# The last half chunk of the delta rule on the attention's tiles, a solve in blocks of 16, and two pads

## Chip, cores, metric

One Trainium2 core runs the whole program. The metric is device microseconds (us) of one execution, with all inputs in HBM at the start and the result in HBM at the end. Engines are named as the profile names them: PE (TensorE matmuls), PEld (its weight loads), DVE (VectorE), ACT (ScalarE), POOL (GpSimd), SP (the queue that issues most DMAs).

## What is computed

One decoder layer over 2048 tokens of width 1024: a normalised input is projected once; a stick-breaking attention of 8 heads and a gated delta rule of 4 heads run side by side; their outputs are projected back, and a feed-forward of width 4096 follows.

```python
h = rmsnorm(x, norm_mix) * (1 + sc_a) + sh_a
proj = h @ w_in                     # q, k, v of the attention; q, k, v, z, a, b of the delta rule
o_a = stick_breaking_attention(q_a, k_a, v_a)
o_b = chunk_gated_delta_rule(q_b, k_b, v_b, g, beta)       # chunks of 64 tokens
x = x + g_a * (concat[o_a, rmsnorm(o_b) * silu(z)] @ w_out)
h = rmsnorm(x, norm_mlp) * (1 + sc_m) + sh_m
x = x + g_m * (relu(h @ w_ff1)^2 @ w_ff2)
# in the delta rule, for each head and chunk of 64 tokens:
a_mat = tril(k_beta @ k.T * decay, -1) + eye               # 64 x 64
t_mat = triangular_solve(a_mat, eye)                       # its inverse
```

## The kernel before

**Stages.** The sequence is cut into four chunks of 512 tokens, taken from c = 3 down to c = 0. For each one, `project(c)` multiplies the normalised input by the input weights (PE, tiles `mmk`, `mmv`, `mmq`, `mmK`, `mmQ`, `mmV`, `mmz`), `decay_terms(c)` prepares the decays, `delta_half(c, 1)` and `delta_half(c, 0)` run the delta rule over 256 tokens each, and `attention(c)` runs 4 pairs of heads in 2 groups each. `attention_far(c)` then reads a flag from the chip (line 567) and branches: the far keys are needed only if some weight hasn't died out. `outs(c)` (tiles `mmo`) is the output projection of a chunk: outs(3) runs in chunk 1, outs(2) beside chunk 0, outs(1) and outs(0) behind it. The feed-forward then takes tokens in two halves of 1024, first chunks 2 and 3: `load_h` makes the operand tiles `b..`, `ff1` multiplies w_ff1 by them (lines 1151 to 1153), `ff2` multiplies w_ff2 by the tiles `hidh`, `hidl` that `split` makes (lines 1210 to 1212). Each float32 product is three float32r matmuls (high by high, high by low, low by high) of 512 columns.

**Order.** Nothing is ordered by hand. A scheduler orders the instructions by their place in the program and what they depend on, and `tc.high_priority(offset=800)` moves a block's instructions up by 800 places. Each engine then runs its own list strictly in that order. Tiles of one tag share its buffers: a tile waits until an earlier user of the buffer is done.

**Tiles and pools.** On the right side of SBUF lie the pools `at` (the attention's tiles: `sn`, `ald`, `sp`, `aT0`, `aT1`, `qf`, `rkb`, `av`, `om`) and below it `dn` (the delta rule's: `dd`, `kw`, `ktok`, `mt`, `bv`, `AT`, `wq` and others, one buffer a tag, `cv` three). When chunk 0 is done, `right.close()` frees both, and the pool `fb` with the feed-forward's `b..` tiles (112 KB) takes the same room. Its tiles wait one by one for the tiles that they lie on. On the left lie `cp`, `wp` (weights: `ws`, `wh`, `wl`) and `act` (activations), then smaller pools, and in their room later the feed-forward's.

**Addresses.** The trace doesn't show them; they follow from the pools and sizes. Counted in bytes past a multiple of 256, tiles start in the kernel before at: `wp`, `act`, `hidh`, `hidl`: 32; the `b..` tiles and `at`: 224; most of `dn`: 64; `wab` (line 433): 128.

**A half chunk.** `delta_half` transposes k (line 720, `kt`), forms the lower matrix `mt` (lines 756, 758) for two blocks p = 1, 0 of 128 tokens, packs the 32 x 32 diagonal blocks into `Gt` (line 762) and transposes them into `M` (line 776). The **solve** (lines 787 to 793) inverts all of them at once on DVE: 31 steps of two or four small instructions each, 116 in a half chunk. `XT` and `xt` put the inverses back (lines 795, 798), eight transposes fill the block diagonal `xbd` (line 802). `pz` and `px` (lines 839, 845) join pairs of 32 to 64 on PE, `pw` and `pu` apply the inverse, and a recursion of four steps follows (lines 868 to 889), with a norm and the transfer to `mix_d` at the end (lines 892 to 907).

Of the kernel before, what the change touches and what calls it, by code (L numbers as in the profile page):

```python
# [16 lines left out]
P = 128  # L17
# [10 lines left out]
DH = 4  # L28
# [13 lines left out]
C_MASK = C_XI + 8 * 32  # L42
# [10 lines left out]
NVEC = 115  # L53
# [3 lines left out]
def tile_hybrid_layer(  # L57
# [23 lines left out]
    mx, pms, inner, right = [ctx.enter_context(ExitStack()) for _ in range(4)]  # L81
# [50 lines left out]
    if True:  # L132
# [7 lines left out]
        pq = inner.enter_context(tc.tile_pool(name="pq", bufs=2, space=PSUM))  # L140
        at = sb("at", 1, right, "right")
# [489 lines left out]
        for t in xbd + vz:  # L631
            G.memset(t, 0.0)
# [51 lines left out]
        def delta_half(c, hf, terms):  # L684
# [9 lines left out]
            def tile2(tag, name, bufs=1):  # L694
                return dn.tile(bc, F32, tag=tag, name=f"{name}{nm}", bufs=bufs)
# [7 lines left out]
            dd = [tile2(f"dd{p}", f"dd{p}_") for p in range(2)]  # L703
# [47 lines left out]
            Gt = dn.tile([P, 32, 2, DH], F32, tag="Gt", name=f"Gt{nm}")  # L751
# [23 lines left out]
            M = dn.tile([P, 32, 32], F32, tag="M", name=f"M{nm}")  # L775
            V.transpose(M, Gt.rearrange("q i p h -> q i (p h)").unsqueeze(2).to_broadcast([P, 32, 4, 8]))
            X = dn.tile([P, 8, 32], F32, tag="X", name=f"X{nm}")
            nc.sync.dma_start(X.rearrange("p a i -> p (a i)"), consts[:, C_XI:C_MASK])
            Xv = X.rearrange("p (e o) i -> p o e i", o=2)
            tm = dn.tile([P, 2, 80], F32, tag="tm", name=f"tm{nm}")  # L780
            for j in range(31, 0, -1):
                a0 = j // 4
                todo = []
                for o in range(2):
                    e0 = (a0 - o + 1) // 2
                    ne = 4 - e0
                    if ne:
                        todo.append((Xv[:, o, e0:4], tm[:, o, 0:ne * j].rearrange("p (e i) -> p e i", e=ne), ne))
                for x, t, ne in todo:
                    V.tensor_tensor(t, x[:, :, j:j + 1].to_broadcast([P, ne, j]),  # L790
                                    M[:, 0:j, j].unsqueeze(1).to_broadcast([P, ne, j]), ALU.mult)
                for x, t, ne in todo:
                    V.tensor_tensor(x[:, :, 0:j], x[:, :, 0:j], t, ALU.subtract)
            XT = dn.tile([P, 8, 4, 2, DH], F32, tag="Gt", name=f"XT{nm}")
            V.transpose(XT.rearrange("q a g p h -> q a (g p h)"), X)
            xt = [dn.tile([P, DH, 8, 4], F32, tag=f"xt{p}", name=f"xt{p}_{nm}") for p in range(2)]
            for p in (1, 0):
                (A.copy if p else G.tensor_copy)(xt[p], XT[:, :, :, p, :].rearrange("q a g h -> q h a g"))
                xt[p] = xt[p].rearrange("q h a g -> q h (a g)")
# [25 lines left out]
            wq = [dn.tile([P, DH, 2, P], F32, tag=f"wq{p}", name=f"wq{nm}_{p}") for p in range(2)]  # L825
# [7 lines left out]
            for p in (1, 0):  # L833
# [7 lines left out]
                for a in range(2):  # L841
                    lo, hi = slice(64 * a, 64 * a + 32), slice(64 * a + 32, 64 * a + 64)
                    ps = bank(f"px{nm}_{p}{a}", [P, DH, 32], "s")
                    for h in range(DH):
                        T.matmul(ps[hi, h, :], lhsT=zt[lo, h, :], rhs=xbd[p][lo, h, lo], start=True, stop=True)
                    A.activation(xbd[p][hi, :, lo], ps[hi], AF.Copy, scale=-1.0)
# [183 lines left out]
        for c in range(NCH - 1, -1, -1):  # L1030
# [210 lines left out]
def _layout(inputs):  # L1241
# [30 lines left out]
    xi = np.zeros((P, 8, 32), np.float32)  # L1272
    for p in range(P):
        for a in range(8):
            xi[p, a, 4 * a + p % 32 // 8] = 1
    cst[:, C_XI:C_MASK] = xi.reshape(P, 256)
# [47 lines left out]
```

## Time and profile before

| | us |
|---|---|
| median of 3 runs | 2852.66 |
| lowest, highest | 2842.65, 2853.85 |
| the profiled execution | 2854.61 |
| its span in the trace | 2852.8 |
| granted TensorE clock, mean of the span | 0.964 |

The span splits at 1497 us: before it lies everything up to the output projection, behind it the feed-forward, in which PE is busy without a break but for one stretch around 2150 us. A row "line engine op out<-in xcount" names the line of the kernel, the tile written and the tiles read; "idle before" is the time that the engine stood still ahead of it, with what ended that.

### The profile page before, as it was taken

To read this page: it belongs to the slowest core of one execution; us is meant where nothing else is said; L and a number is where in the kernel's file an instruction comes from. 1 tells how busy PE (TensorE), PEld (TensorE's weight loads), DVE (VectorE), ACT (ScalarE), POOL (GpSimd) and SP (SyncE) were. 2 spreads that over 40 slices of the span, in tenths; PEclk is the share of its full clock that TensorE was granted. 3 is DMA by queue.
4 is the path that set the end of the run, shared out by engine and by line. 5 is a ranking of instruction groups with operands and counts; after the bars stand their busy time and mean duration, and the time that the engine had idled before them with its cause. 6 is when DMAs were issued, how large, how long until landed. Compare 5 with 4: busy or idle time off the path is not lost.

```text
span 2852.8 us, 37490 instructions
## 1 busy us (share of the span) xinstructions
PE 2631.5 (92%) x13044; PEld 2135.1 (75%) x13044; DVE 1775.0 (62%) x4290; ACT 1165.0 (41%) x2263; POOL 659.5 (23%) x525
## 2 busy tenths in 40 slices
PE   4898789899979999799859999999998999999999
PEld 2687568777868778677648888888876888888887
DVE  7664993588346873568566556555668555555655
ACT  4553443154415452354344343344345343344332
POOL 3222300121002100022253222222226222222221
PEclk9999889999989999898979999999999999999999
DMA  8786786565556556554342111111024111111012
GB/s 308 265 311 207 251 293 208 183 191 176 184 158 205 182 176 189 158 181 138 122 161 94 59 60 42 48 60 60 30 100 166 60 59 43 47 60 60 30 60 89
DMA packets 219089, 390.21 MB, mean 137 GB/s; under 512 B 21944, under 2 KB 68984, under 8 KB 214776
## 3 DMA queue, kind: packets, MB, share of 16 engines
q1 hardware_dynamic: 200696, 358.16, 38.8%
q10 hardware_dynamic: 18176, 29.37, 2.8%
q8 instruction: 110, 1.80, 0.3%
q14 instruction: 107, 0.88, 0.1%
HBM read 302.94 MB, written 84.51 MB: 136 GB/s over the span
## 4 chain that ended last, share of the span: by engine, by line
PE 47%; DVE 2%; DMA 2%; issue 1%; POOL 1%; ACT 0%; SPq 0%; DVEq 0%; POOLq 0%; ACTq 0%
PE f L1210 8%; PE f L1211 8%; PE f L1212 8%; PE f L1151 7%; PE f L1152 7%; PE f L1153 7%; DMA fx<-x_d 1%; DVE fx L1067 0%; DVE bl L130 0%; PE mmo L216 0%; PE mmo L218 0%; PE mmo L217 0%; DVE y L1215 0%; DMA mx<-mix_d 0%; DMA rs_d<-acc 0%
## 5 line engine op out<-in xcount | busy, mean ns | idle before, releaser
L1215 DVE SCALAR_TENSOR_TENSOR y<-f,mods,y 128x512 f32<-128x512 f32 x512 | 363.6, 746 | 249.3 <-PE f L1212 249.1
L1210 PE MATMUL f<-hidh,wh 128*128 128x512 f32 x1024 | 401.5, 393 | 7.1 <-DVE y L1215 7.1
L1211 PE MATMUL f<-hidl,wh 128*128 128x512 f32 x1024 | 401.8, 393 | 3.2 <-POOL hidl L1193 3.2
L1212 PE MATMUL f<-hidh,wl 128*128 128x512 f32 x1024 | 381.2, 392 | 0.8 <-POOL wl L173 0.8
L1151 PE MATMUL f<-bh,swh 128*128 128x512 f32 x896 | 354.9, 396 | 16.6 <-ACT swh L1144 16.6
L1152 PE MATMUL f<-bl,swh 128*128 128x512 f32 x896 | 354.3, 395 | 0.0
L1153 PE MATMUL f<-bh,swl 128*128 128x512 f32 x896 | 347.4, 395 | 0.0
L1210 PEld LDWEIGHTS f<-hidh,wh 128*128 128x128 f32 x1024 | 193.7, 189 | 54.1 <-DVE y L1215 11.4
L1211 PEld LDWEIGHTS f<-hidl,wh 128*128 128x128 f32 x1024 | 193.8, 189 | 44.7 <-POOL hidl L1193 4.4
L1212 PEld LDWEIGHTS f<-hidh,wl 128*128 128x128 f32 x1024 | 193.4, 189 | 42.7 <-POOL wl L173 1.3
L1151 PEld LDWEIGHTS f<-bh,swh 128*128 128x128 f32 x896 | 168.4, 188 | 57.9 <-ACT swh L1144 17.0
L172 ACT CAST wh<-ws 128x512 fp32r<-128x512 f32 x128 | 79.5, 621 | 301.1 <-PE f L1211 245.6
L1152 PEld LDWEIGHTS f<-bl,swh 128*128 128x128 f32 x896 | 168.4, 188 | 41.6 <-issue 0.2
L1153 PEld LDWEIGHTS f<-bh,swl 128*128 128x128 f32 x896 | 168.1, 188 | 41.2
L1193 POOL TENSOR_TENSOR hidl<-t,hidh 128x512 fp32r<-128x512 f32 x64 | 101.6, 1587 | 335.6 <-ACT hidh L1192 316.0
L1144 ACT CAST swh<-wa 128x512 fp32r<-128x512 f32 x96 | 59.4, 622 | 263.0 <-PE f L1152 258.9
L1165 DVE TENSOR_TENSOR t<-t,f 128x512 f32<-128x512 f32 x128 | 87.4, 683 | 121.8 <-PE f L1153 88.8
L1137 POOL TENSOR_TENSOR sws<-wa 128x512 f32<-128x512 f32 x64 | 90.4, 1412 | 307.6 <-DVE wl L173 285.2
L1145 DVE TENSOR_TENSOR swl<-sws,swh 128x512 fp32r<-128x512 f32 x128 | 144.9, 1133 | 20.7 <-ACT swh L1144 20.6
L1145 DVE TENSOR_TENSOR swl<-wa,swh 128x512 fp32r<-128x512 f32 x96 | 86.3, 901 | 94.5 <-ACT swh L1144 94.5
L173 POOL TENSOR_TENSOR wl<-ws,wh 128x512 fp32r<-128x512 f32 x52 | 67.6, 1301 | 248.8 <-ACT wh L172 248.4
L1166 ACT ACTIVATE t<-t 128x512 f32<-128x512 f32 x128 | 80.9, 632 | 81.2 <-DVE t L1165 81.2
(354 smaller groups left out, 5866.1 us busy)
## 6 DMA issues: line engine op xcount, KB each, us to landing
wa<-in_w_ff_dram SPq DMA_DIRECT2D x32, 1024.0 KB
ws<-in_w_ff_dram SPq DMA_DIRECT2D x128, 256.0 KB
wada<-in_w_ada_dram SPq DMA_DIRECT2D x48, 512.0 KB
wso<-in_w_out_dram SPq DMA_DIRECT2D x64, 256.0 KB
cv_d<-ev SPq DMA_DIRECT2D x48, 256.0 KB
cv<-cv_d SPq DMA_DIRECT2D x24, 512.0 KB
x<-in_xc_dram SPq DMA_DIRECT2D x40, 256.0 KB
mx<-mix_d SPq DMA_DIRECT2D x32, 256.0 KB
```

Of the source, the lines that this page charges most:

```text
L1137: G.tensor_tensor(t, x, y, op)
L1145: V.tensor_tensor(wl, x, wh.bitcast(F32), SUB)
L1151: T.matmul(ps, lhsT=wh[:, k, :], rhs=ah, start=first and k == 0, stop=False, skip_group_check=True)
L1152: T.matmul(ps, lhsT=wh[:, k, :], rhs=al, start=False, stop=False, skip_group_check=True)
L1153: T.matmul(ps, lhsT=wl[:, k, :], rhs=ah, start=False, stop=stop and k == 3, skip_group_check=True)
L1165: V.tensor_tensor(t, t, ps, op)
L1166: A.activation(t, t, AF.Relu)
L1193: (G if i % 2 else V).tensor_tensor(hl, x, hh.bitcast(F32), SUB)
L1210: T.matmul(ps[n], lhsT=wh[:, s], rhs=ah, start=j == 0, stop=False)
L1211: T.matmul(ps[n], lhsT=wh[:, s], rhs=al, start=False, stop=False)
L1212: T.matmul(ps[n], lhsT=wl[:, s], rhs=ah, start=False, stop=j == 1)
L1215: V.scalar_tensor_tensor(ys[m][:, cs], ps[n], mods[:, 40 + m:41 + m], ys[m][:, cs], ALU.mult, ALU.add)
```

## The change

- The order for chunk 0: `delta_half(0, 1)`, `attention(0)`, `attention_far(0)`, then `delta_half(0, 0)`, in place of both half chunks ahead of the attention. Both keep the offset of 800.
- In that last half chunk, `dd`, `kw`, `ktok`, `mt`, `bv`, `AT` and `wq` are taken from tags of `at` (the dict `free`); all other tiles stay in `dn`.
- In all eight half chunks the solve inverts 16 x 16 blocks: two of them lie side by side in `M`, selected by two 0/1 columns of `vecs`; 15 steps of two instructions; then pairs of 16 are joined to 32 on PE (`py`, `pv`), with more copies on ACT and four whole transposes on DVE, while `xbd` is filled by ACT.
- Two pads of 56 floats (224 bytes) for a partition: `pad` at the start of `cp` on the left, `edge` at the outer end of the right side, which stays until the end of the program. With them and the new tile sizes tiles start, past a multiple of 256, at: `wp`, `act`, `hidh`, `hidl`: 0; the `b..` tiles: 0; `at` but for its first tile: 0; `dn`: 224.

```diff
-C_MASK = C_XI + 8 * 32
+C_MASK = C_XI + 8 * 16
...
-NVEC = 115
+V_E0 = 115
+NVEC = 117
...
+    cp.tile([P, 56], F32, name="pad")
...
+        edge = right_pad.enter_context(tc.tile_pool(name="edge", bufs=1, side="right"))
+        edge.tile([P, 56], F32, name="edge")
         at = sb("at", 1, right, "right")
         dn = sb("dn", 1, right, "right")
...
+        yz = [dn.tile([P, DH, 32], F32, name=f"yz{i}") for i in range(2)]
...
+            free = {"mt1": ("aT0", 1), "mt0": ("aT1", 1), "bv1": ("av", 2), "bv0": ("av", 2), "AT1": ("ald", 2),
+                    "AT0": ("ald", 2), "ktok1": ("qf", 2), "ktok0": ("qf", 2), "kw1": ("om", 1), "kw0": ("rkb", 1),
+                    "wq1": ("sp", 2), "wq0": ("sp", 2)} if (c, hf) == (0, 0) else {}
...
+                if tag in free:
+                    return at.tile(shape, F32, tag=free[tag][0], name=f"{name}{nm}", bufs=free[tag][1])
...
+            if free:
+                dd = at.tile([P, 2, DH, P], F32, tag="sn", name=f"dd{nm}")
+                dd = [dd[:, p] for p in range(2)]
...
-                    (A.copy if p else G.tensor_copy)(Gt[q, :, p, :], mt[p][q, :, q].rearrange("q h i -> q i h"))
+                    for e in range(2):
+                        (A.copy if p else G.tensor_copy)(Gt[q, :, e, p, :],
+                                                              mt[p][q, :, 32 * d + 16 * e:32 * d + 16 * e + 16]
+                                                              .rearrange("q h i -> q i h"))
...
+            M = dn.tile([P, 16, 32], F32, tag="M", name=f"M{nm}")
+            V.transpose(M, Gt.rearrange("q i e p h -> q i (e p h)").unsqueeze(2).to_broadcast([P, 16, 2, 16]))
+            e0, e1 = vecs[:, V_E0:V_E0 + 1], vecs[:, V_E0 + 1:V_E0 + 2]
+            V.tensor_scalar(M[:, :, 16:32], M[:, :, 16:32], e1, None, ALU.mult)
+            V.scalar_tensor_tensor(M[:, :, 0:16], M[:, :, 0:16], e0, M[:, :, 16:32], ALU.mult, ALU.add)
...
+            for j in range(15, 0, -1):
+                n = 8 - j // 2
+                x, t = X[:, j // 2:], tm[:, 0:n * j].rearrange("p (e i) -> p e i", e=n)
+                V.tensor_tensor(t, x[:, :, j:j + 1].to_broadcast([P, n, j]),
+                                M[:, 0:j, j].unsqueeze(1).to_broadcast([P, n, j]), ALU.mult)
+                V.tensor_tensor(x[:, :, 0:j], x[:, :, 0:j], t, ALU.subtract)
+            Xw = dn.tile([P, 8, 32], F32, tag="Xw", name=f"Xw{nm}")
+            V.tensor_scalar(Xw[:, :, 0:16], X, e0, None, ALU.mult)
+            V.tensor_scalar(Xw[:, :, 16:32], X, e1, None, ALU.mult)
...
             for p in (1, 0):
...
+                for e in range(2):
+                    A.copy(xt[p][:, :, 16 * e:16 * e + 16].rearrange("q h (a g) -> q h a g", g=2),
+                           XT[:, :, :, e, p, :].rearrange("q a g h -> q h a g"))
+                turned(xr[p], xt[p])
+                ps = bank(f"py{nm}_{p}", [P, DH, 16], "s")
                 for d in range(4):
                     q = slice(32 * d, 32 * d + 32)
-                    V.transpose(xbd[p][q, :, q], xt[p][q])
+                    for h in range(DH):
+                        T.matmul(ps[q, h, :], lhsT=mt[p][q, h, q], rhs=xt[p][q, h, 16:32], start=True, stop=True)
+                A.copy(yz[p][:, :, 16:32], ps)
+                ps = bank(f"pv{nm}_{p}", [P, DH, 16], "s")
...
+                        T.matmul(ps[q, h, :], lhsT=yz[p][q, h, :], rhs=xr[p][q, h, 0:16], start=True, stop=True)
+                V.tensor_tensor(xr[p][:, :, 0:16], xr[p][:, :, 0:16], ps, ALU.subtract)
+                turned(xt[p], xr[p])
+                for d in range(4):
+                    q = slice(32 * d, 32 * d + 32)
+                    A.copy(xbd[p][q, :, q], xr[p][q])
...
                 delta_half(c, 1, terms)
-                delta_half(c, 0, terms)
+                if c:
+                    delta_half(c, 0, terms)
             with tc.high_priority(offset=800 if c == 0 else 1):
                 carry = attention(c)
             attention_far(c, carry)
+            if c == 0:
+                with tc.high_priority(offset=800):
+                    delta_half(c, 0, terms)
```

## Rows read from the trace of the kernel before

**Rows 1.** the page, section 1: busy us, share of span, instructions
```profile
PE 2631.5 (92%) x13044; PEld 2135.1 (75%) x13044; DVE 1775.0 (62%) x4290; ACT 1165.0 (41%) x2263; POOL 659.5 (23%) x525
```

**Rows 2.** busy time by stretch: from:to, length, busy (instructions), PEclk, DMA share, GB/s
```profile
300.00:350.00 50.00, 34.77 (x171) 26.81 (x170) 44.62 (x126) 20.28 (x55) 10.04 (x11) 0.84 0.83 272
...
350.00:400.00 50.00, 42.14 (x185) 31.27 (x183) 46.81 (x194) 20.58 (x41) 0.00 (x0) 0.82 0.78 261
...
1300.00:1350.00 50.00, 44.29 (x210) 34.79 (x211) 45.04 (x171) 24.27 (x64) 15.42 (x14) 0.83 0.45 144
...
1400.00:1450.00 50.00, 27.23 (x134) 22.25 (x133) 29.27 (x72) 13.61 (x20) 10.69 (x8) 0.80 0.26 83
...
1450.00:1500.00 50.00, 31.87 (x123) 24.69 (x122) 35.59 (x30) 22.36 (x30) 34.95 (x23) 0.81 0.57 189
...
1550.00:1600.00 50.00, 50.00 (x222) 40.65 (x221) 29.71 (x54) 16.32 (x29) 12.45 (x9) 1.00 0.14 43
```

**Rows 3.** waits of PE, 250 to 1400 us: us in total, times, longest
```profile
PE mmz L218 <- DMA wlz<-wm_d: 18.7, 4, 7.6
...
PE vt L720 <- DVE mt L758: 12.9, 2, 6.8
...
PE pa L538 <- DVE sp L528: 10.2, 5, 4.6
...
PE vt L720 <- DVE bv L771: 8.7, 3, 5.4
```

**Rows 4.** stretches from matmul to matmul: lines 433, 216 (1.2 GHz), ff1, ff2
```profile
84.11:87.64 3.53, 3.52 (x16) 2.08 (x16) 1.97 (x4) 1.58 (x2) 0.44 (x1) 1.00 0.83 275
...
728.36:732.20 3.84, 3.84 (x10) 2.97 (x9) 2.15 (x5) 2.67 (x5) 0.00 (x0) 0.50 0.01 3
...
1606.28:1622.85 16.57, 16.57 (x72) 13.28 (x71) 10.09 (x13) 9.66 (x17) 4.53 (x4) 1.00 0.38 128
...
1623.08:1637.15 14.07, 14.07 (x63) 11.64 (x62) 7.91 (x11) 3.11 (x5) 4.78 (x4) 1.00 0.00 0
```

**Rows 5.** instructions of single lines: ns min/median/max, first and last start
```profile
L790 DVE TENSOR_TENSOR tm<-X,M x464: 119/201/261, 167.2 to 1360.8; 128x24 f32<-128x24 f32 x15, 128x30 f32<-128x30 f32 x11, 128x27 f32<-128x27 f32 x10, 128x28 f32<-128x28 f32 x9
...
L793 DVE TENSOR_TENSOR X<-X,tm x464: 146/184/1311, 167.4 to 1361.0; 128x24 f32<-128x24 f32 x15, 128x30 f32<-128x30 f32 x11, 128x27 f32<-128x27 f32 x10, 128x28 f32<-128x28 f32 x9
...
L776 DVE STREAM_TRANSPOSE M<-Gt x8: 1232/1241/1245, 165.5 to 1326.5; 128x1024 f32<-128x1024 f32 x8
...
L802 DVE STREAM_TRANSPOSE xbd<-xt x64: 289/302/308, 189.8 to 1364.3; 32x128 f32<-32x128 f32 x64
```

**Rows 6.** the view of rows 2, DVE alone: the one solve that ran alone
```profile
165.40:188.70 23.30, 23.07 (x135) 1.00 0.95 332
```

**Rows 7.** the chain that ended last, in order of time: start, us, what
```profile
1362.83 0.52 PE pz L839 x16
...
1390.71 0.89 PE pu L854 x8
...
1429.37 2.58 DMA mix_d<-sz
...
1491.32 4.83 DMA wa<-in_w_ff_dram
...
1496.89 0.80 PE f L1151
```

**Rows 8.** instructions in order of time, PE, ACT and DVE around the branch
```profile
1172.59 2.08 PE L509 MATMUL z<-akf,qf 64*128 64x256 f32 x8 [6.33 <-DVE akf L488]
...
1300.36 0.26 ACT L729 ACTIVATE kt<-kt 128x128 f32<-128x128 f32 x1
...
1331.76 1.98 PE L549 MATMUL po<-aT,av 128*64 128x256 f32 x12
...
1334.08 0.28 DVE L564 TENSOR_REDUCE flag<-pf 1x1 f32<-1x128 f32 x1
...
1339.19 0.32 DVE L793 TENSOR_TENSOR X<-X,tm 128x46 f32<-128x46 f32 x2 [2.53 <-DVEq L567]
```

More of the change, by code (lines that the diff above doesn't have):

```diff
@@ L79, in tile_hybrid_layer @@
     dr = ctx.enter_context(tc.tile_pool(name="dr", bufs=1, space=DRAM))
-    mx, pms, inner, right = [ctx.enter_context(ExitStack()) for _ in range(4)]
+    right_pad, mx, pms, inner, right = [ctx.enter_context(ExitStack()) for _ in range(5)]
     wp = mx.enter_context(tc.tile_pool(name="wp", bufs=3))
@@ L630, in tile_hybrid_layer @@
         vz = [dn.tile([P, DH, P], F32, name=f"vz{i}") for i in range(2)]
-        for t in xbd + vz:
+        yz = [dn.tile([P, DH, 32], F32, name=f"yz{i}") for i in range(2)]
+        for t in xbd + vz + yz:
             G.memset(t, 0.0)
@@ L702, in delta_half @@
                               row_d[c][2 * hf:2 * hf + 2].rearrange("b h t -> (b h t)").partition_broadcast(P))
-            dd = [tile2(f"dd{p}", f"dd{p}_") for p in range(2)]
+            if free:
+                dd = at.tile([P, 2, DH, P], F32, tag="sn", name=f"dd{nm}")
+                dd = [dd[:, p] for p in range(2)]
+            else:
+                dd = [tile2(f"dd{p}", f"dd{p}_") for p in range(2)]
             for p in (1, 0):
@@ L750, in delta_half @@
             mt = [tile2(f"mt{p}", f"mt{p}_") for p in range(2)]
-            Gt = dn.tile([P, 32, 2, DH], F32, tag="Gt", name=f"Gt{nm}")
+            Gt = dn.tile([P, 16, 2, 2, DH], F32, tag="Gt", name=f"Gt{nm}")
             for p in (1, 0):
@@ L781, in delta_half @@
[L781 to L793, printed above, removed]
@@ new lines, in delta_half @@
+            tm = dn.tile([P, 64], F32, tag="tm", name=f"tm{nm}")
+            for j in range(15, 0, -1):
[5 more added lines that the diff above has]
+            Xw = dn.tile([P, 8, 32], F32, tag="Xw", name=f"Xw{nm}")
@@ new lines, in delta_half, with turned @@
+            V.tensor_scalar(Xw[:, :, 0:16], X, e0, None, ALU.mult)
+            V.tensor_scalar(Xw[:, :, 16:32], X, e1, None, ALU.mult)
+            XT = dn.tile([P, 8, 2, 2, 2, DH], F32, tag="Gt", name=f"XT{nm}")
+            V.transpose(XT.rearrange("q a g e p h -> q a (g e p h)"), Xw)
+            xt = [dn.tile([P, DH, 32], F32, tag=f"xt{p}", name=f"xt{p}_{nm}") for p in range(2)]
+            xr = [dn.tile([P, DH, 32], F32, tag=f"xr{p}", name=f"xr{p}_{nm}") for p in range(2)]
+            def turned(o, x):
+                V.transpose(o.rearrange("q h i -> q (h i)"), x.rearrange("q h i -> q (h i)"))
@@ L800, in delta_half @@
+            for p in (1, 0):
+                for e in range(2):
[3 more added lines that the diff above has]
+                ps = bank(f"py{nm}_{p}", [P, DH, 16], "s")
                 for d in range(4):
                     q = slice(32 * d, 32 * d + 32)
-                    V.transpose(xbd[p][q, :, q], xt[p][q])
+                    for h in range(DH):
[4 more added lines that the diff above has]
+                    q = slice(32 * d, 32 * d + 32)
+                    for h in range(DH):
+                        T.matmul(ps[q, h, :], lhsT=yz[p][q, h, :], rhs=xr[p][q, h, 0:16], start=True, stop=True)
+                V.tensor_tensor(xr[p][:, :, 0:16], xr[p][:, :, 0:16], ps, ALU.subtract)
+                turned(xt[p], xr[p])
+                for d in range(4):
+                    q = slice(32 * d, 32 * d + 32)
+                    A.copy(xbd[p][q, :, q], xr[p][q])
@@ L824, in delta_half @@
                 V.tensor_scalar(rqs[64 - 64 * a:128 - 64 * a], rq[64 * a:64 * a + 64], float(P) ** -0.5, None, ALU.mult)
-            wq = [dn.tile([P, DH, 2, P], F32, tag=f"wq{p}", name=f"wq{nm}_{p}") for p in range(2)]
+            wq = [tile2(f"wq{p}", f"wq{p}_", shape=[P, DH, 2, P]) for p in range(2)]
             for p in (1, 0):
@@ L844, in delta_half @@
                     for h in range(DH):
-                        T.matmul(ps[hi, h, :], lhsT=zt[lo, h, :], rhs=xbd[p][lo, h, lo], start=True, stop=True)
+                        T.matmul(ps[hi, h, :], lhsT=zt[lo, h, :], rhs=xr[p][lo, h, :], start=True, stop=True)
                     A.activation(xbd[p][hi, :, lo], ps[hi], AF.Copy, scale=-1.0)
@@ L1271, in _layout @@
     cst[:, C_MASK:] = np.where(i[None, :] > i[:, None], 0.0, -1e30)
-    xi = np.zeros((P, 8, 32), np.float32)
+    xi = np.zeros((P, 8, 16), np.float32)
     for p in range(P):
         for a in range(8):
-            xi[p, a, 4 * a + p % 32 // 8] = 1
-    cst[:, C_XI:C_MASK] = xi.reshape(P, 256)
+            xi[p, a, 2 * a + p % 32 // 16] = 1
+    cst[:, C_XI:C_MASK] = xi.reshape(P, 128)
+    vec[:, V_E0 + 1] = i // 8 % 2
+    vec[:, V_E0] = 1 - vec[:, V_E0 + 1]
     def tiles(w, n):
```

15 lines of the change are left out of this document (3 added, 12 removed).

## Prediction

> **What bounds the kernel now.** I read the page's busy times first: PE is busy for 2631.5 of 2852.8 us and DVE for 1775 [rows 1]. A busy PE is not a PE at its best, so the stretches come next [rows 2]. The reader is to see two regimes. Behind 1500 us PE is full, at the full clock level of 2.4 GHz, with DVE at 30 of 50 us: there only the spacing of the matmuls counts. Ahead of 1497 us PE is the bound in most stretches, but loses time where it waits in its own order for a chain on other engines. From 300 to 400 us DVE is busy for 45 and 47 of 50 us and PE stands still for 23 of 100. From 1400 to 1500 us PE is busy for 59 of 100 only. The waits of PE between [rows 3] are for weights by DMA (18.7 us in `mmz`), for `mt` (12.9), for the attention's `sp` (10.2) and for `bv` (8.7), each in a few long pieces. The chain of waits [rows 7] shows what sets the end of the first part: the last half chunk writes `mix_d` at 1429.4; from there to the first feed-forward matmul at 1496.9 are 67.5 us of output projection and `load_h`, whose tiles lie on those of `at` and `dn`.
>
> **1. The pads and the stream of matmuls.** A run of 72 matmuls of `ff1` takes 16.57 us, so 16.57 / 71 = 233.4 ns from start to start; 63 matmuls of `ff2` take 14.07 us, so 14.07 / 62 = 226.9 ns [rows 4]. Both are 512 columns with weights of `wp`, at the same clock. What differs is where the moving tile starts: `ff1` reads `b..` at 224 while its weights start at 32, `ff2` reads `hid` at 32 with weights at 32. The 16 matmuls of line 433 have moving tiles at 32 and weights at 128 and take 3.53 / 15 = 235.3 ns, though their weights are 64 columns wide. So the equal start has the shorter spacing, twice. With the pads all of them start at 0. I take 226.9 ns for both: ff1 has 2 halves x 16 groups x 7 products x 12 = 2688 matmuls, so 2688 x (233.4 - 226.9) = **-17.5 us**, all of it on the path, since PE doesn't stop there [rows 2]. The rest of the path there keeps its 226.9. Bounds: 0, if it isn't the start that makes the difference, and far more, if an even start (0, not 32) is worth something by itself. For that end the row at 1.2 GHz gives a price: 3.84 / 9 = 426.7 ns [rows 4], which is 512 columns with nothing added; half of it is 213.4 ns, a floor. This is a rival, below.
>
> The Trainium skill speaks against this part: TensorE: Matmul & The Clock Gate, in "Step-by-step: what each phase is for", gives PE two independent read ports, one for the moving operand and one for the weights, so that their places shouldn't matter to each other; by it the pads would give 0 here. The trace disagrees so far, with 233.4 against 226.9 ns.
>
> **2. The solve, in every half chunk.** Removed on DVE: 58 pairs of instructions at 201 and 184 ns, 22.3 us; `M` at 1.24; eight transposes at 0.302, 2.4 [rows 5]; with `XT` (0.445, unchanged) 26.4 us. That fits the one solve that ran alone, 23.07 us busy in 23.30 [rows 6] without `xbd`. Added on DVE, by the nearest rows: 30 instructions at the same 192 ns, 5.8 us; `M` of half the size 0.6; two masks of `M` and two of `Xw` at 0.2 to 0.45, say 1.3; `XT` 0.45; four whole transposes between 0.30 and 0.45, 1.4; two subtractions 0.5. Sum 10. So **-16 us of DVE** each, 130 over eight. Added on PE: 64 matmuls of 32 x 32 x 16. `pz` shows 16 records in 0.52 us for 8 matmuls [rows 7], two records each; 128 records at 33 ns are 4.2 us, 34 over eight. Added on ACT: some 15 small copies more, estimated from the 0.26 to 0.42 us of those there now at 5 us; ACT is busy for four tenths and hides it, unless PE waits for one of them: `pv` needs `yz`, and everything queued behind `pv` on PE waits with it. The POOL copies double in number and halve in size.
>
> What is that worth up to chunk 0? PE is bound, so 6 x 4.2 = 25 us more work come on the path where PE is full, perhaps 20 of them. Against it stand the waits for DVE: 23 us from 300 to 400 us, and `mt`, `sp` and `bv` elsewhere [rows 2, 3], in all some 50 us in which DVE is late, of which half the solve's 16 us per half chunk can buy back; the DMA waits stay. I take +20 - 30 = **-10 us**, between +25 (nothing is bought back) and -45 (all, with the matmuls in gaps).
>
> **3. The last half chunk.** Now it waits for tiles: its `kt` squares of p = 0 come at 1300.4, when the first half chunk's `ktok` is free [rows 8], its `M` at 1326.5 [rows 5], its solve takes until 1361.2 with the branch's 2.5 us of standing DVE in it [rows 8], `pz` to `pu` last from 1362.8 to 1391.6, the recursion and the norm until 1429.4 [rows 7]: 129 us. After the change it doesn't wait for the other half chunk, but for the attention and, by `qf`, `om`, `rkb`, `sn`, `ald` and `sp`, which the far branch also uses, for the branch. The attention's 8 groups run from 1172.6 to 1333.7, 20 us each; the branch lets go at 1339.2 [rows 8]. With nothing of the last half chunk between them, and 16 us less solve on DVE at 1150 to 1190, I take 18 us a group: 1172.6 + 144 + 5 = 1322 (bounds 1306 at 16 us a group, 1339 as now). From there: both blocks' `kt`, norms, `mt`, `Gt` 24 (26 now for one block, among the attention's groups), solve and joining 20 (38 now, to the end of `xbd`), `pz` to `pu` 25 (29), recursion, norm and transfer 37: 106 us, with 95 and 120 as bounds. End at 1322 + 106 = 1428, against 1429.4: **-2 us**, between -28 and +30. What of PE's work can hide there is spent either way: outs(2) goes before the branch, outs(1) (192 matmuls, 44 us) beside the chain. `load_h` gains nothing: its first `b` tiles lie on `S`, `vz`, `o` and on tiles of `at`, all alive until the recursion ends, so the 67.5 us behind stay. Queued behind the wait: on SP the `rb`, `cv` and `sz` loads of the half chunk stand ahead of weights for outs(1) and of `fx`; PE and ACT hold outs(1) behind a late step for a microsecond or two, as they do now.
>
> **4. Small things.** The memset of `yz`, the smaller constant `X` and wider `vecs` lie beside other work at the start: 0, and under 1 us if not. Pads make DMA targets in `wp`, `at` and `fa` start at 0; in the feed-forward DMAs are far from the bound, ahead of it I take 0, at most a few us in the first 200.
>
> **Sum.** 2854.6 (the profiled execution; span 2852.8) - 17.5 - 10 - 2 = 2825; its execution lies 2 us over the median of the runs, so 2823. Because the unknown ends of part 1 lie below, and the order is made anew with more freedom, I round to **2820 us**.
>
> **The rivals.**
> - *The stream reaches its floor.* An even start takes the added 13 to 20 ns away altogether: 3072 x (226.9 - 213.4) + 2688 x (233.4 - 213.4) = 41 + 54 = 95 us in the feed-forward, and 3072 matmuls of `mm*` x 13.5 ns, seven tenths on the path, 29 more; in place of 17.5. 2823 - 107 = 2716; half of it, 2770. For it: at 1.2 GHz nothing is added. Against it: `hid` and its weights already have equal starts and still show 13.5 ns, and I have no row with an even one for 512 columns. The Trainium skill, TensorE: Matmul & The Clock Gate, "Back-to-back issue gap", would set N / 2.4 + 2.5 = 216 ns; no row here shows it. Chance 0.2.
> - *The pads do nothing*: another cause separates ff1 from ff2. 2823 + 17 = 2840. Chance 0.15.
> - *Slower: the last half chunk becomes the longer end.* It can't start before the branch. If the attention keeps its 20 us a group, the branch ends at 1339, and if the chain takes 120 us among the matmuls of outs(1), the end is at 1459, +30; with the 34 us of small matmuls two thirds exposed (+22), no DVE wait bought back, and -17.5 for the stream: 2854 + 34 = about 2888. It decides where its first `kt` on PE comes after 1429 - 106 = 1323. For it: all its steps are in a row and PE serves it in its own order; against it: DVE has room there. Chance 0.1.
>
> **How the numbers follow.** The forecast has 0.5, the others 0.2, 0.15 and 0.1, 0.05 is for what I don't see. Around the forecast parts 2 and 3 give about ±25. The range reaches down to 2735, into the first rival, and up to 2862. A measurement can tell some 0.5%, 14 us: under 2838 lie nearly all of the forecast, the first rival and half of the second: 0.75 faster, 0.17 the same, 0.08 slower.
>
> **What the profile after will show.** Right: windows in ff1 with 226 to 228 ns a matmul, and ff2 unchanged; 30 instructions of the solve in a half chunk, DVE's busy time 120 to 140 us lower; the first `kt` of the last half chunk on PE at about 1320, `mix_d` at about 1425, the feed-forward's first matmul 65 to 70 us behind it. Wrong: ff1 still at 233 (no effect of the pads) or both near 214 to 220 (the floor), a feed-forward that starts after 1510 (the slower end), or PE waits for `yz` and `xr` that add up to over 10 us.

## The result and the profile after

The changed kernel took 2879.6 us (median of 4 runs, 2874.5 to 2885.2), the kernel before 2851.5 us in the same comparison: ratio 1.0106, 95% interval 1.0081 to 1.0132, so **1.06% slower**. The forecast was 2820 us in a range from 2735 to 2862: wrong in sign and outside the range. The profiled execution of after has a span of 2883.4 us, 30.6 more than that of before.

The page, section 1, of after (busy us, share of the span, instructions), against [rows 1]:

```profile
PE 2658.9 (92%) x14068; PEld 2173.8 (75%) x14068; DVE 1711.6 (59%) x3618; ACT 1176.0 (41%) x2387; POOL 662.1 (23%) x551
```

PE has 1024 records more and 27 us more work. They are the joining's 512 small matmuls, two records each as the prediction counted them; where this text and the expectations count small matmuls (256, 1024, 2048), they count records. DVE has 672 instructions fewer and is busy for 63 us less. Where the 30.6 us are is seen from two marks on PE. One is the last matmul of `mmz`, behind which PE has only attention, delta rule and output projection left; the other is the first matmul of the feed-forward. The view of one line gives them as the last and the first start (columns: count, ns min/median/max, first to last start, forms). Before, whose first `f` is in [rows 7]:

```profile
L218 PE MATMUL mmz<-h,wlz x128: 387/389/797, 250.7 to 1238.5; 128*128 128x512 f32 x128
```

After:

```profile
L223 PE MATMUL mmz<-h,wlz x128: 388/389/795, 258.1 to 1261.8; 128*128 128x512 f32 x128
...
L1196 PE MATMUL f<-bh,swh x896: 389/389/793, 1543.9 to 2833.3; 128*128 128x512 f32 x180
```

I call the part up to the first mark the **front**, from there to the second the **tail**. Front 1238.5 -> 1261.8: +23.3. Tail 1496.9 - 1238.5 = 258.4 -> 1543.9 - 1261.8 = 282.1: +23.7. Feed-forward 2852.8 - 1496.9 = 1355.9 -> 2883.4 - 1543.9 = 1339.5: -16.4. The sum is 30.6: the stream of matmuls gave what it promised, and both parts ahead of it lost more.

The windows of after (columns as in [rows 2]) show the tail and the feed-forward:

```profile
1350.00:1400.00 50.00, 48.55 (x221) 37.68 (x222) 25.00 (x55) 26.64 (x59) 19.42 (x17) 1.00 0.50 165
...
1400.00:1450.00 50.00, 40.23 (x353) 33.53 (x353) 26.79 (x104) 19.43 (x62) 7.63 (x13) 0.80 0.19 60
...
1450.00:1500.00 50.00, 27.43 (x125) 22.12 (x125) 30.87 (x72) 14.31 (x20) 12.98 (x10) 0.75 0.28 89
...
1500.00:1550.00 50.00, 33.17 (x125) 25.77 (x124) 35.01 (x30) 20.86 (x28) 34.83 (x22) 0.81 0.57 198
...
1700.00:1750.00 50.00, 50.00 (x222) 41.42 (x221) 27.28 (x36) 21.48 (x38) 11.41 (x9) 1.00 0.25 80
```

The hole in PE that lay from 1400 to 1500 us before [rows 2] now reaches to 1550: 40, 27 and 33 us busy of 50 at a mean granted clock of 0.75 to 0.81. In the feed-forward PE is full in both kernels.

The waits of PE in after, 250 to 1540 us (us in total, times, longest), for [rows 3]:

```profile
PE py L832 <- ACT xt L825: 13.1, 3, 10.1
...
PE pz L880 <- DVE xt L821: 7.1, 1, 7.1
...
PE vt L738 <- DVE mt L776: 7.0, 1, 7.0
...
PE mmz L223 <- DMA wlz<-wm_d: 5.2, 2, 4.7
...
PE mmz L221 <- DMA whz<-wm_d: 3.9, 1, 3.9
```

Some of the old waits shrank: `mmz` for its weights from 18.7 to 5.2 and 3.9, `vt` for `mt` from 12.9 to 7.0. In their place stand waits of the new joining: `py` for `xt` 13.1, `pz` for `xt` 7.1. One of them in detail, DVE and then PE in order of time:

```profile
551.38 0.88 DVE L493 SCALAR_TENSOR_TENSOR akf<-akf,gqk,rkb 128x640 f32<-128x640 f32 x1 [10.81 <-DMA rkb<-rk_d]
552.18 0.21 DVE L839 TENSOR_TENSOR xr<-xr,pv 128x64 f32<-128x64 f32 x1
552.43 0.31 DVE L821 STREAM_TRANSPOSE xt<-xr 128x128 f32<-128x128 f32 x1
```

```profile
552.80 0.63 PE L880 MATMUL pz<-xt,mt 32*32 32x32 f32 x8 [7.12 <-DVE xt L821]
```

DVE stands 10.8 us before `akf` of the attention, which wants `rkb` by DMA. The subtraction `xr` of the joining is behind it in DVE's order, and `pz` on PE waits 7.1 us for the turned `xt`. The old solve needed no other engine between `M` and `xbd` but for one copy; the new one goes DVE, ACT, DVE, PE, ACT, PE, DVE, and can stand behind something on each.

The chain that ended last in after, for [rows 7]:

```profile
1381.85 0.97 ACT dd L726 x2
...
1427.73 1.34 PE py L832 x32
...
1432.47 1.16 PE pv L838 x29
...
1444.11 1.48 PE pu L895 x8
...
1477.22 2.29 DMA mix_d<-sz
```

The recursion's result `mix_d` leaves at 1477.2, 47.9 us later than before, and the feed-forward starts 66.7 us behind it (67.5 before).

### The profile page after: what moved, and what is told of

It is laid out like the page before. It is cut to its first block, busy times and chain, and to the rows that moved or that the text cites. A ratio compares the mean times of both kernels' runs of the same rounds, so it can differ in the third digit from the quotient of the medians.

```text
span 2883.4 us, 39062 instructions
## 1 busy us (share of the span) xinstructions
PE 2658.9 (92%) x14068; PEld 2173.8 (75%) x14068; DVE 1711.6 (59%) x3618; ACT 1176.0 (41%) x2387; POOL 662.1 (23%) x551
## 4 chain that ended last, share of the span: by engine, by line
PE 44%; DVE 3%; issue 1%; DMA 1%; POOL 1%; ACT 1%; SPq 0%; ACTq 0%; POOLq 0%; DVEq 0%
PE f L1255 8%; PE f L1256 8%; PE f L1257 7%; PE f L1198 7%; PE f L1196 6%; PE f L1197 6%; DVE bl L132 1%; DMA fx<-x_d 0%; DVE y L1260 0%; DVE fx L1112 0%; DMA mx<-mix_d 0%; DVE swl L1190 0%; PE mmo L223 0%; DMA wa<-in_w_ff_dram 0%; PE mmo L221 0%
## 5 line engine op out<-in xcount | busy, mean ns | idle before, releaser
L1196 PEld LDWEIGHTS f<-bh,swh 128*128 128x128 f32 x896 | 169.2, 189 | 54.2 <-ACT swh L1189 18.7
L869 POOL TENSOR_TENSOR wq<-cv,rb 128x256 f32<-128x256 f32 x32 | 24.7, 793 | 440.4 <-DMA kf_d<-ev 140.1
L525 DVE TENSOR_TENSOR_SCAN pb<-sn 128x256 f32<-128x256 f32 (+1 forms) x128 | 90.8, 720 | 56.6 <-ACT sn L522 56.2
```

What stands on the lines that cost most here:

```text
L525: V.tensor_tensor_scan(pb[:, j, hd, 1:w + 1], sn[:, j, hd, 0:w], sn[:, j, hd, 0:w], 1.0, ALU.mult, ALU.bypass)
L1196: T.matmul(ps, lhsT=wh[:, k, :], rhs=ah, start=first and k == 0, stop=False, skip_group_check=True)
```

## The experiments

All times are medians; "before" in the same comparisons lay between 2849.5 and 2852.0 us. Front and tail are read from one profiled execution of each kernel, by the two marks. The front of before, 1238.5, is itself on the long side: the kernels whose front is unchanged (pads alone, move alone, order alone, pads and move) show 1227.7 to 1233.0, and I take 1230 as the level to compare with. Marks of single executions scatter by up to 11 us (1227.7 to 1238.5 where nothing ahead of them was changed), so a difference in a mark is read where it is well above that, or where the medians bear it out. As the order is made anew for each kernel, some instructions can also stand on the other side of a mark.

| kernel | us | ratio, 95% interval | front | tail |
|---|---|---|---|---|
| pads alone | 2832.9 | 0.9943 (0.9915 to 0.9971) | 1227.9 | 258.0 |
| move alone | 2863.4 | 1.0042 (1.0027 to 1.0058) | 1227.7 | 270.1 |
| order alone, old tiles | 2861.9 | 1.0049 (1.0027 to 1.0071) | 1233.0 | 273.1 |
| pads and move | 2841.7 | 0.9959 (0.9945 to 0.9974) | 1230.2 | 268.8 |
| solve alone | 2879.8 | 1.0093 (1.0062 to 1.0125) | 1260.6 | 270.3 |
| pads and solve | 2861.8 | 1.0037 (1.0018 to 1.0056) | 1259.2 | 265.1 |
| solve, 2048 small matmuls | 2912.2 | 1.0215 (1.0176 to 1.0253) | 1290.3 | 266.0 |
| solve, 256 | 2853.0 | 1.0007 (0.9994 to 1.0020) | 1230.1 | 267.3 |
| solve, 256, no readers | 2810.9 | 0.9855 (0.9830 to 0.9879) | 1227.6 | 225.1 |
| solve, no joining | 2822.2 | 0.9911 (0.9884 to 0.9937) | 1234.8 | 225.2 |
| solve, 1024 on constants, no readers | 2851.7 | 1.0002 (0.9983 to 1.0020) | 1261.6 | 231.4 |
| solve, 1024, no readers | 2883.8 | 1.0115 (1.0096 to 1.0133) | 1293.2 | 232.4 |
| all three (after) | 2879.6 | 1.0106 (1.0081 to 1.0132) | 1261.8 | 282.1 |

**The parts one by one.** Pads alone:

```diff
+    cp.tile([P, 56], F32, name="pad")
+        edge = right_pad.enter_context(tc.tile_pool(name="edge", bufs=1, side="right"))
+        edge.tile([P, 56], F32, name="edge")
```

> The kernel before with the two pads alone. Theory (the three parts add up, sizes read off the traces of before and after: stream -20, upstream +20, tail +30): ff1 from 233.3 to 226.7 ns a matmul, nothing ahead of the feed-forward changes; 2851 - 18 to 20 = about 2832 us. Rival (the pads move the places of everything and cost something ahead of the feed-forward as well, part of the +20 there): feed-forward 18 us shorter, but its first matmul later than 1497, so 2840 to 2851 us.

Measured 2832.9: -16.6, a little under the theory's 18 to 20. The front is the level named above, the tail that of before (258.4).

The 16-block solve alone, with its joining; order, tiles and pads as before:

```diff
-            for j in range(31, 0, -1):
...
+            for j in range(15, 0, -1):
...
+                ps = bank(f"py{nm}_{p}", [P, DH, 16], "s")
...
+                ps = bank(f"pv{nm}_{p}", [P, DH, 16], "s")
```

> The kernel before with the 16-block solve alone; order, tiles and pads as before. Theory (adds up): the second half of the end of mmz of chunk 0 comes some 20 us later as in the trace of after, because the joining puts 1024 small matmuls on PE and makes DVE, ACT and PE wait for each other; 2851 + 20 = about 2871 us (2860 to 2880). Rival (the prediction's step 2: DVE's time bought back, all of the loss is in the move): 2841 us (2830 to 2851). DVE busy 60 to 70 us lower than before by both.

Measured 2879.8, +30: as much as the whole change costs. The rival, which is the prediction's own step, is out.

The move alone, order and tiles:

```diff
+            free = {"mt1": ("aT0", 1), "mt0": ("aT1", 1), "bv1": ("av", 2), "bv0": ("av", 2), "AT1": ("ald", 2),
...
+                if c:
+                    delta_half(c, 0, terms)
...
+            if c == 0:
+                with tc.high_priority(offset=800):
+                    delta_half(c, 0, terms)
```

> The kernel before with the last half chunk behind the attention and on the attention's tiles alone; old solve, no pads. Theory (adds up): nothing changes ahead of chunk 0, the chain of the last half chunk starts when the branch ends, near 1340, and lasts 106 us plus the 10 to 16 us that the old solve is longer: mix_d at 1455 to 1465, first feed-forward matmul at 1525 to 1535, about 2881 us (2870 to 2895). Rival 1 (all of the loss of after is the move): about 2910 us. Rival 2 (the move loses only together with the new solve, whose chain crosses engines): 2851 us or less, mix_d near 1430.

Measured 2863.4, +14: less than the theory said, more than the second rival. On PE, the first `z` of the last attention and the branch's `pf`, then SP's transfer of `mix_d`:

```profile
1162.41 2.08 PE L509 MATMUL z<-akf,qf 64*128 64x256 f32 x8 [7.21 <-DVE akf L488]
...
1314.68 0.37 PE L562 MATMUL pf<-idon,fmx 128*1 128x128 f32 x1
```

```profile
1430.90 0.38 SPq L918 DMA_DIRECT2D mix_d<-sz  x1
```

```profile
L218 PE MATMUL mmz<-h,wlz x128: 388/390/797, 249.0 to 1227.7; 128*128 128x512 f32 x128
...
L1166 PE MATMUL f<-bh,swh x896: 392/394/797, 1497.8 to 2803.5; 128*128 128x512 f32 x180
```

The attention, freed of the half chunk, takes 1314.7 - 1162.4 = 152 us to `pf`, 9 fewer than before [rows 8]; the chain behind it, with the old solve, another 116. `mix_d` leaves at 1430.9, only 1.5 us later than before [rows 7], but this execution's front is 11 us shorter than that of before, as in the other kernels that don't touch it. Its tail is 270.1, longer by 11.7, about what the medians say.

Pads and solve together, without the move:

> The kernel after with the last half chunk back in its old place and on its old tiles: pads and 16-block solve. Theory (adds up): 2851 - 20 + 20 = about 2851 us (2840 to 2862), so the move is worth +28. Rival (the prediction's steps 1 and 2 hold): 2851 - 18 - 10 = 2823 us (2810 to 2835), and the move alone costs 56.

Measured 2861.8, at the upper end of the theory's range, since the solve alone costs 30 and not 20: by the single parts it should be 2849.5 - 16.6 + 30.4 = 2863.3. The parts add up. So do all three: 2863.3 + 13.9 = 2877.2, and after took 2879.6.

The order alone is the move without `free`: the last two pieces of its diff, on the old tiles.

> The kernel before with the last half chunk issued behind the last attention and its far branch, but on its old tiles; old solve, no pads. Theory (the 14 us that the move alone costs come from its late start, which the attention's tiles cause): the half chunk starts as before when the other one lets go of its tiles, 2850 us (2845 to 2855). Rival (the place in the order itself costs: the attention's and the branch's instructions stand in front of it on each engine): 2863 us, as with the tiles.

Measured 2861.9: the rival. The place in the order costs the 10 to 14 us; the attention's tiles change nothing on top that is clear of the intervals.

Pads and move, with the old solve:

> The kernel after with the old 32-block solve: pads and the moved last half chunk. Theory (the parts add up): 2850 - 17 + 12 = 2845 us. Rival (the move pays with the shorter stream, or costs only with the new solve): 2833 us or less, which would make it the fastest of the correct ones together with the pads alone.

Measured 2841.7, 8.9 over the pads alone. By the ratios to before the intervals of the two overlap; together with the move alone (+14) and the order alone (+10) it says that the move costs without the new solve too.

**The solve: matmuls or hand-overs?** Without its joining:

```diff
                 turned(xr[p], xt[p])
-                ps = bank(f"py{nm}_{p}", [P, DH, 16], "s")
...
-                V.tensor_tensor(xr[p][:, :, 0:16], xr[p][:, :, 0:16], ps, ALU.subtract)
-                turned(xt[p], xr[p])
```

> The kernel before with the 16-block solve, but without its joining: both groups of small matmuls (py, pv), the copy to yz, the subtraction and the second turn are left out, so the off-diagonal 16-blocks of the inverse are missing. Theory W (PE is the bound, the matmuls of the joining lie on its path in full, DVE's saved time buys nothing): the 37 us that py and pv hold PE in the kernel with the solve alone go away, 2880 - 30 to 37, about 2847 us, the same as before. Rival H (the hand-overs between PE, ACT and DVE cost, not the matmuls): also about 2847 us; the next two runs tell these apart. Rival B (the solve on DVE, its masks and copies or the new order are what costs): 2870 to 2880 us. The prediction's step 2 (DVE's saved time buys back waits of 30 us and more): 2815 to 2825 us.

Measured 2822.2: none of the theories of that moment, but the prediction's step 2. The shorter solve on DVE is worth -30, and the joining costs 58.

A quarter of the matmuls, and twice as many:

```diff
-                    for h in range(DH):
-                        T.matmul(ps[q, h, :], lhsT=mt[p][q, h, q], rhs=xt[p][q, h, 16:32], start=True, stop=True)
+                    T.matmul(ps[q, :, :], lhsT=mt[p][q, 0, q], rhs=xt[p][q, :, 16:32], start=True, stop=True)
```

> The kernel before with the 16-block solve, with one matmul of 64 columns a block in py and pv in place of four of 16 (256 small matmuls in place of 1024, the weights of the first head used for all four, so that the joining is wrong for three heads). The chain over PE, ACT and DVE stays. Theory W (matmul time on PE): about 20 of the 26 us that the small matmuls take from start to start go, 2860 us (2855 to 2866). Rival H (hand-overs): 2878 to 2882 us.

```diff
-                    for h in range(DH):
+                    for h in 2 * list(range(DH)):
```

> The kernel before with the 16-block solve, with every small matmul of py and pv issued twice to the same place (2048 in place of 1024). Theory W (matmul time on PE): another 1024 x 26 ns = 26 us, 2906 us (2900 to 2912). Rival H (hand-overs): under 2885 us, since the hand-overs stay as many and the chain gets longer by half a us a time.

Measured 2853.0 and 2912.2: 27 us for 768 matmuls (35 ns each) and 32 us for 1024 (32 ns each). Theory W comes nearer in both runs, but with 26 ns it was too small: it said 2860 and 2906. What is added on PE is paid in full and somewhat more. But 256 matmuls still cost 31 us over none, so W isn't all.

All matmuls, but no reader behind them:

```diff
-                A.copy(yz[p][:, :, 16:32], ps)
-                V.tensor_tensor(xr[p][:, :, 0:16], xr[p][:, :, 0:16], ps, ALU.subtract)
-                turned(xt[p], xr[p])
```

> The kernel before with the 16-block solve; all 1024 small matmuls of the joining are issued, but nothing reads their results (no copy to yz, no subtraction, no second turn), so the joining is left out of the result. The matmuls still wait for xt and xr, but nothing waits for them. Theory (the solve's +28 is -30 for DVE's saved time, +34 for 1024 matmuls at 33 ns on PE, +24 for the hand-overs PE to ACT to PE to DVE to PE): the 24 go, 2822 + 34 = 2856 us (2850 to 2862). Rival (all of the 58 us between the solve without the joining and the solve with it is matmul time and what it displaces; the hand-overs cost nothing): 2880 us.

Measured 2883.8: by the total the rival, and the hand-overs seemed to cost nothing. The two marks tell more: its tail is 232.4 as against 270.3 of the solve alone, so the hand-overs do cost there; but its front is 1293.2, longer by 33 with the same matmuls. The next two take these apart: 256 matmuls without readers, and 1024 on constants without readers.

```diff
-                        T.matmul(ps[q, h, :], lhsT=mt[p][q, h, q], rhs=xt[p][q, h, 16:32], start=True, stop=True)
+                        T.matmul(ps[q, h, :], lhsT=ident[q, q], rhs=ident[q, 0:16], start=True, stop=True)
```

> The kernel before with the 16-block solve, 256 small matmuls of 64 columns in place of 1024, and nothing reads their results (no copy to yz, no subtraction, no second turn; the joining is left out of the result). With readers this count took 2853 us, without any joining 2822. Theory F (hand-overs behind the matmuls cost 22 us as long as the matmuls are few): 2822 + 256 x 33 ns = 2830 us. Rival G (what costs is that the matmuls of the joining wait in PE's order for xt and xr, and the two banks they take; readers cost nothing): 2850 to 2856 us.

> The kernel before with the 16-block solve, 1024 small matmuls whose operands are blocks of the constant identity and whose results nothing reads (the joining is left out of the result): they wait for nothing but their bank, nobody waits for them. The same count took 2884 us where they waited for xt and xr. Theory (pure matmul time at 33 ns each): 2822 + 34 = 2856 us. Rival G (the wait for xt and xr in PE's order costs the other 28): also 2856; if the matmuls cost about 60 ns each by themselves: 2884 us.

Measured 2810.9 (below both) and 2851.7 (the theory). The first is also 11 us below the kernel without any joining, which has less to do, so some 10 us of a difference between two of these kernels may come from the order alone. Side by side, the marks of four kernels. The solve alone:

```profile
L219 PE MATMUL mmz<-h,wlz x128: 387/390/797, 253.6 to 1260.6; 128*128 128x512 f32 x128
...
L1177 PE MATMUL f<-bh,swh x896: 393/394/797, 1530.9 to 2834.2; 128*128 128x512 f32 x180
```

256 matmuls with readers:

```profile
L219 PE MATMUL mmz<-h,wlz x128: 387/390/795, 251.3 to 1230.1; 128*128 128x512 f32 x128
...
L1175 PE MATMUL f<-bh,swh x896: 392/394/796, 1497.4 to 2804.7; 128*128 128x512 f32 x180
```

256 matmuls without readers:

```profile
L219 PE MATMUL mmz<-h,wlz x128: 387/389/628, 241.4 to 1227.6; 128*128 128x512 f32 x128
...
L1172 PE MATMUL f<-bh,swh x896: 393/394/796, 1452.7 to 2756.7; 128*128 128x512 f32 x180
```

1024 matmuls on constants, without readers:

```profile
L219 PE MATMUL mmz<-h,wlz x128: 387/389/632, 253.0 to 1261.6; 128*128 128x512 f32 x128
...
L1174 PE MATMUL f<-bh,swh x896: 393/394/796, 1493.0 to 2796.9; 128*128 128x512 f32 x180
```

Two things separate. **The front goes by the number of matmuls**, with readers or without: 1227.6 to 1234.8 for 0 or 256, 1259.2 to 1261.8 for 1024, 1290.3 for 2048. Seven of the eight half chunks lie there, 896 matmuls, and 30 / 896 = 33 ns each. **The tail goes by the readers**, whatever the number: 225 to 232 without, 265 to 270 with. One kernel doesn't fit, the front of the 1024 matmuls that wait for `xt` and `xr` and are read by nobody. It and the front of the 1024 on constants (PE alone; length, busy, records, granted clock, DMA share, GB/s):

```profile
0.00:1293.20 1293.20, 1149.32 (x7174) 0.92 0.63 203
```

```profile
0.00:1261.60 1261.60, 1124.09 (x7175) 0.94 0.65 208
```

Of the 31.6 us, PE is busy for 25 with the same number of records, at a lower granted clock, and stands still for 6. Why the clock was lower stays open.

The same view of front and tail of the two kernels with 256 matmuls, with readers and then without:

```profile
0.00:1230.10 1230.10, 1093.33 (x6435) 0.95 0.66 213
1230.10:1497.40 267.30, 216.40 (x1098) 0.88 0.48 150
```

```profile
0.00:1227.60 1227.60, 1097.84 (x6502) 0.95 0.65 213
1227.60:1452.70 225.10, 196.93 (x1030) 0.95 0.56 179
```

Of the 42 us that the tail is longer with readers, PE stands still for 23 (50.9 against 28.2) and is busy for 19.5, at a granted clock of 0.88 in place of 0.95 and with 68 records that stand ahead of the mark in the other kernel. The readers' own work is small (`xr` 0.21 and `xt` 0.31 us a block on DVE in the rows at 552 us above). But the order differs as well: in PE's order the last half chunk's first `kt` stands behind 2899 of the 3072 matmuls of the input projections with readers and behind 2719 without, its first `pz` behind all 320 records of `z` with readers and behind 290 without. How much of the 42 us is waiting at the hand-overs, and how much is the order that the scheduler made because of them, these runs don't separate.

Where the readers lengthen the tail is seen on ACT at the first `kt` of the last half chunk's second block. It stands behind the copy into `ktok`, which waits for the half chunk ahead to let go of that tile ([rows 8] for before). 256 matmuls without readers, 256 with, and the solve alone:

```profile
1198.50 0.26 ACT L732 ACTIVATE kt<-kt 128x128 f32<-128x128 f32 x1
```

```profile
1274.95 0.26 ACT L732 ACTIVATE kt<-kt 128x128 f32<-128x128 f32 x1
```

```profile
1308.65 0.26 ACT L732 ACTIVATE kt<-kt 128x128 f32<-128x128 f32 x1
```

Without readers the half chunk ahead lets go at 1198.5; with readers at 1275.0 and 1308.7, around the 1300.4 of before. With the steps across the engines the half chunks lose again what DVE saved, and the last one again has the attention's work around it and ends late. (The order of the program is laid out anew for each kernel, so the pieces between can't be compared one by one.)

**The pads: equal starts, or a start at 0?** The right pad alone, the left pad alone, and a right pad of 48 words in place of 56, which puts `ff1`'s moving tiles at 32, where the weights are:

```diff
+        edge.tile([P, 48], F32, name="edge")
```

> The kernel before with the right pad alone: ff1's moving tiles start at 0, its weights stay at 32 (unequal starts). Theory (equal starts make the shorter spacing): ff1 stays at 233.3 ns a matmul, ff2 at 226.9. Rival (the start of the moving tile counts by itself, and 0 is good where 224 is bad): ff1 226.7 ns.

> The kernel before with the left pad alone: weights and hid start at 0, ff1's moving tiles stay at 224 (unequal starts). Theory (equal starts): ff1 stays at 233.3 ns, ff2 at 226.7. Rival (a moving tile at 224 is the bad one): also 233.3. Third (the weights' start counts, 0 is good): ff1 226.7 ns.

> The kernel before with a right pad of 48 words in place of 56: ff1's moving tiles start at 32, as its weights do (equal starts, not 0). Theory (equal starts): ff1 226.7 ns a matmul, and about 2833 us as with both pads. Rival (a start at 0 is needed): 233.3 ns, about 2851 us.

Each fence is a run of 72 matmuls of `ff1` from the first start to the last (columns as in [rows 4]; the count takes in one neighbour). Moving tile at 0, weights at 32:

```profile
1604.10:1620.68 16.58, 16.58 (x73) 13.34 (x72) 10.10 (x13) 9.68 (x17) 4.57 (x4) 1.00 0.38 127
```

Moving tile at 224, weights at 0:

```profile
1607.22:1623.80 16.58, 16.58 (x73) 13.34 (x72) 10.10 (x13) 9.67 (x17) 4.56 (x4) 1.00 0.38 127
```

Both at 32:

```profile
1601.19:1617.29 16.10, 16.10 (x73) 13.33 (x71) 10.10 (x13) 9.53 (x17) 4.50 (x4) 1.00 0.39 131
```

After, both at 0, and below it 63 matmuls of `ff2`, unchanged from [rows 4]:

```profile
1654.21:1670.31 16.10, 16.10 (x73) 13.33 (x72) 10.10 (x13) 9.53 (x17) 4.50 (x4) 1.00 0.39 131
...
1629.73:1643.79 14.06, 14.06 (x64) 11.64 (x63) 7.30 (x10) 3.11 (x5) 6.14 (x5) 1.00 0.00 1
```

16.57 us from the first start to the last where the starts differ, 16.09 where they are equal, at 0 or at 32 (the windows are rounded outward by up to 0.01): 71 distances of 233.3 and of 226.7 ns. The times go along: 2852.8, 2852.6 and 2832.2 us (one run each). The theory of equal starts holds, and neither 0 nor 224 counts by itself.

The **pads alone**, 2832.9 us, are the fastest of the kernels with the whole computation, faster than before by 0.6% and than after by 1.6%; 48 words on one side do the same in one run.

## Why the prediction was wrong, step by step

**1. Pads: right.** -17.5 forecast, -16.6 measured alone, 226.7 ns for the 226.9 read from [rows 4], and `ff2` as before. The floor rival is out: with all starts at 0 nothing went below 226.7 ns. So is the rival in which the pads do nothing.

**2. The solve: the step that failed**, -10 forecast with +25 as the bound, +30 measured alone. Its terms: the length of one DVE instruction was right, 15 pairs at 198 and 191 ns in place of 58 at 201 and 192, but the old solve was sized too large. Most of its steps work on two halves in turn, and their records overlap, so lengths can't be added up. The busy time of all DVE instructions on `X` (DVE alone, columns as in [rows 6]), before and after:

```profile
0.00:1500.00 1500.00, 135.40 (x936) 0.94 0.63 202
```

```profile
0.00:1500.00 1500.00, 50.41 (x256) 0.93 0.60 196
```

That is 85 us less over eight half chunks; an old solve held DVE for some 17 us, not for 22.3. The stretch of [rows 6], which seemed to bear out the 22.3, isn't one solve alone: 17 of its instructions are other work (`bv`, `wlQ`, `AT`, `dd`, `hss`). The other steps gone and added about cancel, so some 80 us of DVE were there to be saved, not 120 to 140; its busy time fell by 74 us with the solve alone (1775.0 to 1701.4) and by 63 with the whole change, and what took the rest I can't name. What the shorter solve is worth came out at the amount taken, -30 of the -30 put against the matmuls, but that is luck: it was read from waits ahead of chunk 0, and in the front it buys nothing (1234.8 without any joining against the level of 1230), all of it shows in the tail (225 against 258). The matmuls were sized right, 4.2 us a half chunk, and 33 ns each was measured; but all of them lie on the path, about 30 us in the front, where I took 20. The failed sentence is the one on ACT, which "hides it unless PE waits for one of them": I named the wait of `pv` and of all that is behind it, and priced it at nothing. These hand-overs, on PE and on DVE, with the order that the scheduler makes for them, cost 267 - 225 = 42 us of the tail and take back everything that the shorter solve had given. The sign set for them, PE waits for `yz` and `xr` of over 10 us, was too narrow: PE waited 2.3 us for `yz`, but 20 for `xt`. I had read DVE's waits as if each could be shortened by the solve's time, and not asked what the new steps would stand behind.

**3. The last half chunk.** Its chain was sized well: 106 us forecast from where the branch lets go; in after DVE goes on behind the branch at 1379.3, and to `mix_d` it is 1477.2 - 1379.3 = 98. The attention was sized too short: 144 us to `pf` forecast (18 a group), 152 with the move alone, 169 in after. There both its start and its end came late:

```profile
1203.41 0.80 PE L514 MATMUL z<-akf,qf 64*128 64x256 f32 x2 [3.80 <-DVE akf L493]
...
1262.91 0.60 PE L738 MATMUL kt<-idon,cv 128*128 128x128 f32 x4
...
1372.19 0.27 PE L567 MATMUL pf<-idon,fmx 128*1 128x128 f32 x1
```

```profile
1379.26 2.25 DVE L724 SCALAR_TENSOR_TENSOR dd<-rb,gc,cst 128x128 f32<-128x128 f32 x8 [5.78 <-PEq L572]
1381.43 0.67 DVE L756 TENSOR_TENSOR kw<-kt,egc 128x512 f32<-128x512 f32 x1
```

The first `z` at 1203.4 is 31 us later than before [rows 8]: that is the front, longer by the small matmuls. Of the 17 us that the attention then takes over the move alone I can name only the small matmuls of one half chunk (4), the rest stays open. The sign for the slower rival was ill chosen: the first `kt` of the last half chunk stands on PE at 1262.9, ahead of the 1320 forecast and of the 1323 from which that rival was to decide, since it writes a PSUM bank and no tile of `at`. What stands behind the branch is its reader, `kw` on DVE at 1381.4; the other block's `kt` follows at 1388.5. The other sign, a feed-forward that starts after 1510, came true with 1543.9. The move alone costs 10 to 14 us by its place in the order, inside the bounds of -28 to +30, where -2 was taken. That `load_h` would gain nothing was right: 66.7 us for 67.5.

**The rivals.** The slower one, 2888 us with a chance of 0.1, came nearest to 2879.6, and for half of its reasons: the small matmuls exposed and the last half chunk as the longer end; but its chain was 98 us long and not 120, it started late. Its chance was too small, since I put the matmuls' exposure and the branch's delay in one case with a slow chain, though the first two need no third. The **range** ended at 2862, though the worst bounds of parts 2 and 3 together, +25 and +30 with the pads, come to 2854.6 - 17.5 + 25 + 30 - 2 = 2890: it left no room for both to come out badly, and +25 held nothing for hand-overs.

The sum as it came out, from the marks and the single parts: stream -16; small matmuls in the front +30 against a level of 1230 (+23 against the profiled execution of before, whose front was 8 us long); tail -33 for DVE's time, +42 for the readers, +11 for the place of the last half chunk, and some 4 more that only the whole change shows.

## What to carry to other kernels

Where PE was full, work moved onto it was paid in full, here 32 to 35 ns for each small record; the time taken off DVE was worth something only in one stretch, so both have to be read by stretch. A chain that ran on one engine and is made to cross three can be shorter in busy time and still later at its end, as each crossing can wait behind whatever stands in that engine's order; price every hand-over, for instance by leaving out the readers in an experiment, and see then whether the order has changed too. Where records overlap, size a chain by its busy time and not by the sum of their lengths. Take a change of several parts apart first: here 48 or 56 words of padding carried the whole gain, and the rest lost more than that.

## What the runs showed of the hardware

At the full granted clock (1.00) the distance of two 512-column matmuls depended on whether the moving tile and the weights start at the same place modulo 256 bytes: 226.7 ns for 0/0 and 32/32, 233.3 ns for 224/32, 0/32 and 224/0, as means of 71 distances. Whether 256 is the period wasn't tried; 64 is too short, since 224 and 32 are equal by it. A record of a 32 x 32 x 16 matmul lasts 178 ns, but each one (two to a matmul) lengthened PE's path by 32 to 35 ns; the row is that of `py` in the kernel with the solve alone:

```profile
L817 PE MATMUL py<-xt,mt x512: 177/178/232, 177.9 to 1372.6; 32*32 32x16 f32 x171
```
